# Seven-product units of the down projection: other places for their raw blocks, and splits written next to the loads

## The chip, the cores and the metric

The kernel runs on one core of one Trainium2 chip. The metric is the device time of one execution in microseconds; the time given is the median of several runs.

## The reference

One decoder block on x of 256 tokens by 2048 channels, in float32. Cut to what matters here:

```python
mix = token_mixers(x, w_in, ...)                 # GLA and forgetting attention, merged, projected by w_out
x = layer_norm(ALPHA * x + mix, ln1_g, ln1_b)
g = causal_dwconv(x @ w_gate, conv_w, conv_b)    # width 3
h = jax.nn.gelu(g) * (x @ w_up)                  # 256 x 5632
x = layer_norm(ALPHA * x + h @ w_down, ln2_g, ln2_b)
x = x + jax.nn.sigmoid(x @ w_ple_gate) * (p @ w_ple_proj)
```

The change concerns `h @ w_down`: 256 x 5632 times 5632 x 2048.

## The kernel before

All weights but a few pass through one stream of *units*, `wu[u]`, each 128 partitions by 2048 floats (1 MB). A float32 product is made of three products of float32r parts: an operand is *split* into a high part (`hi`, ScalarE's copy) and a low part (`lo`, VectorE's subtraction of the high part). `unit()` hands out the next unit's split parts and, before that, calls `prep()` until the units up to two ahead have been written into the program. `prep` loads a plain unit as two raw blocks of 128 x 1024 into a ring of 4 places (tag `raw`), splits them into `hi` and `lo` tiles (6 places each, tag `hi` and `lo`), and so feeds TensorE.

The down projection runs in two halves (`nh`), each over 22 units of two k-tiles and 1024 output columns, accumulating into four PSUM banks (`banks`, written dn in the trace). In a *plain* unit TensorE makes 24 products of 128 x 512 (`x_mm`, L300). Units listed in `DNW` (12 in the first half, 10 in the second; 1, 2, 4, 5, 7, 8, 10, 11, ...: mostly two, then a plain one) are *seven-product* units: `seven` (L321) multiplies by a Strassen-like scheme with 7 x 3 = 21 products, some into four more banks (`ms`, dn0m and dn1m). For it a unit needs

- block 0 and 1 of the unit (columns 0 to 1023) and block 3 (columns 1536 to 2047), split: `his`, `los`;
- four combinations of blocks, split, in two tiles `ts`: two were made beforehand, during the gate and up projections, by `combine` on VectorE, and stored in DRAM (`tsd`); the other two are made from blocks 0 and 1 in place, by subtracting the second stored combination (the *pair* subtraction, L151);
- sums of h, loaded into the free half of the first `hi` and `lo` tile by `sums[u]` (GpSimd's DMA queue, L1160 and L1161).

Wide tiles come from 15 places of 128 x 2048 (`s8`, tag S8): in this stage hT holds ten of them in the first half (hT0 to hT9, given back one by one in the second half as their last k-tile is used), the residual z2 two from the end of the first half on, the second LayerNorm's gain and offset two, and the rest serves the seven-product units' `raw` and `ts` tiles.

`prep_seven` loads blocks 0 and 1 into the first half of a wide tile `raw` and the two stored combinations into its second half, and block 3 into a ring place (`raws`). It splits block 3 and blocks 0 and 1 (L149) and makes the pair subtraction. The two tiles `ts` are split later by `split_seven` (L162): `unit()` calls it for the unit being handed out and the one after it, behind its calls of `prep()`.

The loads are issued by SyncE (SP), whose instructions stay in the order of the program (`manual_schedule`), so a load that waits for its place holds back those behind it. On ScalarE and VectorE the order is set by the compiler's planner, by priority (mostly the order of the program) among what its own clock holds ready; it also deals out the places. On the chip each engine then runs its queue strictly in that order.

Of the kernel before, what the change touches and what calls it, by code (L numbers as in the profile page):

```python
# [9 lines left out]
F32 = mybir.dt.float32  # L10
F32R = mybir.dt.float32r
# [3 lines left out]
ALU = mybir.AluOpType  # L15
# [4 lines left out]
P = 128  # L20
# [38 lines left out]
def tile_block(ctx: ExitStack, tc: tile.TileContext, wu, xw, wfv, wpp, xT_in, x_in, pT_in, wlr,  # L59
               chan, gnorm, lng, ident_in, mask_in, cmask_in, out):  # L60
    nc = tc.nc
# [4 lines left out]
    ring = ctx.enter_context(tc.tile_pool(name="ring", bufs=4))  # L66
# [14 lines left out]
    def s8(shape, dt=F32, name=None):  # L81
        t = big.tile([P, S8W], dt, tag="S8", name=name)
        n = int(np.prod(shape[1:]))
        t = t[:shape[0], :n]
        if len(shape) == 3:
            return t.rearrange("p (a b) -> p a b", b=shape[2])
        if len(shape) == 4:
            return t.rearrange("p (a b c) -> p a b c", b=shape[2], c=shape[3])
        return t

    def w_tile(tag, dt, name, u):
        if tag == "lo":
            return wide.tile([P, 1024], dt, tag=tag, name=name)
        o = 0 if u in XSTAT else HSTEP
        return wide.tile([P, WH], dt, tag=tag, name=name)[:, o:o + 1024]

    def t1(name):
        return sm.tile([P, 256], F32, tag="t1", bufs=6, name=name)
# [10 lines left out]
    def copy(o, i, scale=1.0):  # L109
        nc.scalar.activation(o, i, AF.Copy, bias=0.0, scale=scale)  # L110
# [14 lines left out]
    n_prep = [0]  # L125
    ready = {}

    sums, half, later = {}, {}, {}
    units7 = [DN0 + nh * (NF // 2) + i for nh in range(2) for i in DNW[nh]]
    tsi = {u: j for j, u in enumerate(units7)}  # L130
    tsd = dr.tile([len(units7), P, 1024], F32, name="tsd")

    def prep_seven(u):
        raw = s8([P, 2048], name=f"raw{u}")
        small = ring.tile([P, 1024], F32, tag="raw", bufs=4, name=f"raws{u}")[:, 0:512]
        nc.sync.dma_start(raw[:, 0:1024], wu[u, :, 0:1024])
        nc.sync.dma_start(small, wu[u, :, 1536:2048])
        nc.sync.dma_start(raw[:, 1024:2048], tsd[tsi[u]])
        his, los = [], []
        for h, b in enumerate((small, raw[:, 0:1024])):  # L140
            hi = w_tile("hi", F32R, f"hi{u}_{h}", u)
            lo = w_tile("lo", F32R, f"lo{u}_{h}", u)
            n = b.shape[1]
            his.append(hi)
            los.append(lo)
            if h == 0:
                sums[u](hi[:, 512:1024], lo[:, 512:1024])
            copy(hi[:, 0:n], b)
            nc.vector.tensor_tensor(lo[:, 0:n], b, hi[:, 0:n].bitcast(F32), ALU.subtract)  # L149
        pair = raw[:, 0:1024].rearrange("p (a b) -> p a b", b=512)  # L150
        nc.vector.tensor_tensor(pair, pair, raw[:, 1536:2048].unsqueeze(1).broadcast_to([P, 2, 512]),  # L151
                                ALU.subtract)
        half[u] = (his, los, raw)

    def split_seven(u):
        his, los, raw = half.pop(u)
        ts = []
        for h in (1, 0):
            t = s8([P, 2, 1024], F32R, name=f"ts{u}_{h}")
            e = raw[:, h * 1024:h * 1024 + 1024]  # L160
            copy(t[:, 0, :], e)
            nc.vector.tensor_tensor(t[:, 1, :], e, t[:, 0, :].bitcast(F32), ALU.subtract)  # L162
            ts.insert(0, t)
        ready[u] = (his, los, ts)

    def prep():
        u = n_prep[0]
        n_prep[0] += 1
        if u in sums:
            prep_seven(u)  # L170
            return
        his, los = [], []
        for h in range(2):
            raw = ring.tile([P, 1024], F32, tag="raw", bufs=4, name=f"raw{u}_{h}")
            nc.sync.dma_start(raw, wu[u, :, h * 1024:(h + 1) * 1024])
            hi = w_tile("hi", F32R, f"hi{u}_{h}", u)
            c = nc.scalar.activation(hi, raw, AF.Copy, bias=0.0, scale=1.0)  # L177
            if h == 0 and u > DN0:
                tc.keep_in_program_order(c)
            lo = w_tile("lo", F32R, f"lo{u}_{h}", u)  # L180

            def rest(lo=lo, raw=raw, hi=hi):
                return nc.vector.tensor_tensor(lo, raw, hi.bitcast(F32), ALU.subtract)  # L183

            if u in LATE_LO:
                later.setdefault(u, []).append(rest)
            elif u in PIN_LO:
                tc.keep_in_program_order(rest())
            else:
                rest()  # L190
            his.append(hi)
            los.append(lo)
        ready[u] = (his, los)
# [4 lines left out]
    def unit(ahead=3):  # L198
        u = n_used[0]
        n_used[0] += 1  # L200
        while n_prep[0] < min(NU, u + ahead):
            prep()
        for v in (u, u + 1):
            if v in half:
                split_seven(v)
        return ready.pop(u)


# [134 lines left out]
    def x_half(name, act, K, evac, pulls=0, head=0, tail=0, mid=None, done=None, end=None,  # L343
# [9 lines left out]
        def mm(i, w, toks, cs=(0, 1), part=None):  # L353
            for j in range(2):
                kt = 2 * i + j
                x_mm(banks, (w[0][j], w[1][j]), act[kt // 4][:, kt % 4, :], toks,
                     kt == 0, kt == K - 1, cs, part)

        us = [unit() for _ in range(head)]
        for t in range(2):  # L360
            for i, w in enumerate(us):
                mm(i, w, (t,))
        for i in range(head, n - tail):
            if i in ws:
                if i == ws[0]:
                    ms.extend(mmtile(f"{name}m{j}") if j % 2 == 0 else mxtile(f"{name}m{j}")
                              for j in range(4))
                seven(banks, ms, unit(), act, 2 * i, i == ws[0], i == ws[-1])
                if i == ws[-1]:
                    joined(ms)  # L370
            else:
                mm(i, unit(), (0, 1))
            pull(pulls)
            if mid is not None and i in mid:
                mid[i]()
# [121 lines left out]
    for t in range(2):  # L497
        for c, (o, n) in enumerate(fch):
            n = min(n, 1024 - o)
# [144 lines left out]
    for nm, dst, sc in (("fq", fq, P ** -0.5), ("fk", fk, 1.0)):  # L644
        if nm == "fk":
            mixers.append(fox_gen())
        for n in range(8):
            if nm == "fk" and n == 4:
                load_consts2()
            hi, lo = unit()  # L650
# [8 lines left out]
    for nm, dst, sc in (("q", gq, 1.0 / 16.0), ("k", gk, 1.0)):  # L659
        for n in range(8):  # L660
            hi, lo = unit()
            ps = mmtile(f"ps{nm}{n}")
            w_unit(ps, hi, lo, xT, range(16), True, True)
            h, c = n // 2, n % 2
# [163 lines left out]
    for n in range(32):  # L828
        hi, lo = unit()
# [15 lines left out]
    for n in range(16):  # L845
        hi, lo = unit()
# [343 lines left out]
    for n in range(NF):  # L1190
# [22 lines left out]
        u = t1("up")  # L1213
# [168 lines left out]
```

## Time and profile before

| | us |
|---|---|
| runs | 1665.45, 1667.3, 1673.34 (median 1667.3) |
| the profiled execution, its time | 1664.02 |
| its span, first to last instruction | 1662.2 |
| TensorE busy in the span | 1649.7 (99%) |
| VectorE, ScalarE busy | 1206.7 (73%), 871.6 (52%) |
| DMA, mean over the span | 230 GB/s |
| down projection, both halves | 1327.3 to 1554.5 |
| landing of a load from tsd, issue to landing, median | 8.1 |

A row of the table of windows gives the stretch, its length, then busy time and count for TensorE, its weight loads, VectorE, ScalarE and GpSimd, then the granted TensorE clock, the DMA share and GB/s. A row of a timeline gives start, duration, engine, line and operation, the tiles it writes and reads, and in brackets how long the engine was idle before it and what ended that. A row of waits gives who waited for whom, the total, the number of waits and the longest.

### The profile page before, as it was taken

How to read it: one execution, taken by the hardware profiler on the slowest of the kernel's cores; microseconds unless marked ns; L12 is line 12 of the kernel's file. 1: busy time of each engine (PE TensorE's matmuls, PEld its weight loads, DVE VectorE, ACT ScalarE, POOL GpSimd, SP SyncE). 2: the span in 40 equal slices, each digit the busy share in tenths (PEclk: the TensorE clock that was granted, in tenths of full speed). 3: DMA queues.
4: the chain of work that ended last, by engine and by line, in shares of the span. 5: the costliest groups of instructions: out<-in, count | busy, mean ns of one | idle time of the engine just before them, and what ended most of it. 6: DMA issues, size and time to landing. Idle time of an engine off the chain costs nothing.

```text
span 1662.2 us, 24249 instructions
## 1 busy us (share of the span) xinstructions
PE 1649.7 (99%) x8968; PEld 1431.4 (86%) x8968; DVE 1206.7 (73%) x1771; ACT 871.6 (52%) x1255; POOL 92.8 (6%) x213
## 2 busy tenths in 40 slices
PE   9999999999999999999999999999999999999998
PEld 9988888888888888888898888888888877877887
DVE  6666658768756657775688788888777778878774
ACT  6745445445556545444465455555555556456643
POOL 0000000000000000000010121111000111010000
PEclk9999999999999999999999999999999999999999
DMA  7765555555555555658647899988666588689364
GB/s 296 234 202 179 165 189 179 177 179 178 184 179 174 170 190 193 195 194 291 226 150 252 310 349 336 354 322 294 225 205 207 191 292 319 251 320 344 133 209 171
DMA packets 105799, 382.69 MB, mean 230 GB/s; under 512 B 12312, under 2 KB 13216, under 8 KB 104272
## 3 DMA queue, kind: packets, MB, share of 16 engines
q1 hardware_dynamic: 96144, 347.38, 61.1%
q0 software_dynamic: 9392, 33.57, 5.2%
q8 instruction: 70, 1.15, 0.3%
q14 instruction: 49, 0.40, 0.1%
q10 hardware_dynamic: 144, 0.20, 0.0%
HBM read 358.02 MB, written 23.08 MB: 229 GB/s over the span
## 4 chain that ended last, share of the span: by engine, by line
PE 94%; DMA 3%; DVE 1%; SPq 1%; issue 1%; ACT 0%; POOL 0%; DVEq 0%; ACTq 0%
PE psu L256 9%; PE psg L256 9%; PE psm L256 7%; PE dn L300 6%; PE gr L300 5%; PE gv L300 5%; PE wo L300 5%; PE pg L300 5%; PE psu L258 5%; PE psg L258 5%; PE psm L258 4%; PE psa L256 3%; PE fv L462 3%; DMA raw<-tsd 3%; PE psfq L256 2%; PE psfk L256 2%
## 5 line engine op out<-in xcount | busy, mean ns | idle before, releaser
L183 DVE TENSOR_TENSOR lo<-raw,hi 128x1024 fp32r<-128x1024 f32 x524 | 639.1, 1223 | 321.3 <-ACT hi L177 320.0
L177 ACT ACTIVATE hi<-raw 128x1024 fp32r<-128x1024 f32 x524 | 553.0, 1059 | 526.7 <-issue 138.6
L256 PE MATMUL psu<-x1T,hi 128*128 128x512 f32 x688 | 236.0, 389 | 0.0
L256 PE MATMUL psg<-x1T,hi 128*128 128x512 f32 x672 | 230.6, 389 | 0.0
L258 PE MATMUL psu<-x1T,lo 128*128 128x256 f32 x688 | 190.2, 276 | 0.0
L258 PE MATMUL psg<-x1T,lo 128*128 128x256 f32 x672 | 185.9, 277 | 0.0
L256 PE MATMUL psm<-xT,hi 128*128 128x512 f32 x512 | 175.8, 391 | 0.0
L256 PEld LDWEIGHTS psu<-x1T,hi 128*128 128x128 f32 x688 | 129.3, 188 | 26.4
L256 PEld LDWEIGHTS psg<-x1T,hi 128*128 128x128 f32 x672 | 126.3, 188 | 25.9
L258 PE MATMUL psm<-xT,lo 128*128 128x256 f32 x512 | 141.7, 277 | 0.0
L258 PEld LDWEIGHTS psu<-x1T,lo 128*128 128x128 f32 x688 | 129.2, 188 | 0.0
L258 PEld LDWEIGHTS psg<-x1T,lo 128*128 128x128 f32 x672 | 126.1, 188 | 0.3 <-DVE lo L183 0.3
L256 PEld LDWEIGHTS psm<-xT,hi 128*128 128x128 f32 x512 | 96.2, 188 | 19.6
L300 PE MATMUL dn<-hi,hT 128*128 128x512 f32 x352 | 98.1, 390 | 0.0
L258 PEld LDWEIGHTS psm<-xT,lo 128*128 128x128 f32 x512 | 96.2, 188 | 0.1
L256 PE MATMUL psa<-oT,hi 128*128 128x512 f32 x256 | 87.8, 389 | 0.0
L300 PEld LDWEIGHTS dn<-hi,hT 128*128 128x128 f32 x352 | 66.0, 188 | 13.6
L300 PE MATMUL gv<-hi,xT 128*128 128x512 f32 x256 | 72.3, 394 | 0.0
L300 PE MATMUL gr<-hi,xT 128*128 128x512 f32 x256 | 72.2, 394 | 0.0
L258 PE MATMUL psa<-oT,lo 128*128 128x256 f32 x256 | 70.8, 276 | 0.0
L300 PE MATMUL wo<-hi,mT 128*128 128x512 f32 x256 | 69.9, 390 | 0.0
L300 PE MATMUL pg<-hi,x2T 128*128 128x512 f32 (+1 forms) x256 | 68.3, 378 | 0.0
(307 smaller groups left out, 2960.6 us busy)
## 6 DMA issues: line engine op xcount, KB each, us to landing
raw<-in_wu_dram SPq DMA_DIRECT2D x546, 512.0 KB, 4.7
comb<-in_wu_dram SPq DMA_DIRECT2D x22, 768.0 KB, 8.9
tsd<-comb POOLq DMA_DIRECT2D x22, 512.0 KB, 7.7
raw<-tsd SPq DMA_DIRECT2D x22, 512.0 KB, 8.1
fvraw<-in_wfv_dram SPq DMA_DIRECT2D x15, 524.0 KB, 7.8
raws<-in_wu_dram SPq DMA_DIRECT2D x22, 256.0 KB, 7.1
hi<-hsd POOLq DMA_DIRECT2D x22, 256.0 KB, 5.4
lo<-hsd POOLq DMA_DIRECT2D x22, 256.0 KB, 6.0
```

What stands on the lines that cost most here:

```text
L177: c = nc.scalar.activation(hi, raw, AF.Copy, bias=0.0, scale=1.0)
L183: return nc.vector.tensor_tensor(lo, raw, hi.bitcast(F32), ALU.subtract)
L256: nc.tensor.matmul(ps, lhsT=hi[i // 8 if hoff == 0 else 0][:, w0 % 1024:w0 % 1024 + P], rhs=a[:, kt % 4, :], start=first and i == 0, stop= ...
L258: nc.tensor.matmul(ps[:, 256:512], lhsT=lo[i // 8 if hoff == 0 else 0][:, w0 % 1024:w0 % 1024 + P], rhs=a[:, kt % 4, 0:256], start=False, ...
L300: nc.tensor.matmul(bs[j][:, 0:m], lhsT=x, rhs=v[:, o:o + m], start=first and i == 0, stop=last and i == 2)
L462: nc.tensor.matmul(fbk[t][c][:, 0:n], lhsT=x, rhs=w[:, o:o + n], start=kt == 0 and i == 0, stop=kt == 15 and i == 2)
```

## The change

For a seven-product unit, blocks 0 and 1 are loaded into a ring place (`low`, 128 x 1024) and the stored combinations and block 3 into a wide place (`top`, 128 x 1536), in the order blocks 0 and 1, combinations, block 3. `split_seven` and its calls in `unit()` go away; the two `ts` tiles are split at the end of `prep_seven`, the untouched second one first.

```diff
     def prep_seven(u):
-        raw = s8([P, 2048], name=f"raw{u}")
-        small = ring.tile([P, 1024], F32, tag="raw", bufs=4, name=f"raws{u}")[:, 0:512]
-        nc.sync.dma_start(raw[:, 0:1024], wu[u, :, 0:1024])
-        nc.sync.dma_start(small, wu[u, :, 1536:2048])
-        nc.sync.dma_start(raw[:, 1024:2048], tsd[tsi[u]])
-        his, los = [], []
-        for h, b in enumerate((small, raw[:, 0:1024])):
+        low = ring.tile([P, 1024], F32, tag="raw", bufs=4, name=f"raw{u}")
+        top = s8([P, 1536], name=f"top{u}")
+        nc.sync.dma_start(low, wu[u, :, 0:1024])
+        nc.sync.dma_start(top[:, 0:1024], tsd[tsi[u]])
+        nc.sync.dma_start(top[:, 1024:1536], wu[u, :, 1536:2048])
+        his, los, ts = [], [], []
+
+        def split(hi, lo, b):
+            copy(hi, b)
+            nc.vector.tensor_tensor(lo, b, hi.bitcast(F32), ALU.subtract)
+
+        def sevenths(h, b):
+            t = s8([P, 2, 1024], F32R, name=f"ts{u}_{h}")
+            split(t[:, 0, :], t[:, 1, :], b)
+            ts.insert(0, t)
+
+        for h, b in enumerate((top[:, 1024:1536], low)):
...
-            copy(hi[:, 0:n], b)
-            nc.vector.tensor_tensor(lo[:, 0:n], b, hi[:, 0:n].bitcast(F32), ALU.subtract)
-        pair = raw[:, 0:1024].rearrange("p (a b) -> p a b", b=512)
-        nc.vector.tensor_tensor(pair, pair, raw[:, 1536:2048].unsqueeze(1).broadcast_to([P, 2, 512]),
+            split(hi[:, 0:n], lo[:, 0:n], b)
+        pair = low.rearrange("p (a b) -> p a b", b=512)
+        nc.vector.tensor_tensor(pair, pair, top[:, 512:1024].unsqueeze(1).broadcast_to([P, 2, 512]),
                                 ALU.subtract)
-        half[u] = (his, los, raw)
-
-    def split_seven(u):
...
+        sevenths(1, top[:, 0:1024])
+        sevenths(0, low)
         ready[u] = (his, los, ts)
...
         while n_prep[0] < min(NU, u + ahead):
             prep()
-        for v in (u, u + 1):
-            if v in half:
-                split_seven(v)
         return ready.pop(u)
```

More of the change, by code (lines that the diff above doesn't have):

```diff
@@ L126, in tile_block @@
     ready = {}
-    sums, half, later = {}, {}, {}
+    sums, later = {}, {}
     units7 = [DN0 + nh * (NF // 2) + i for nh in range(2) for i in DNW[nh]]
@@ L147, in prep_seven @@
                 sums[u](hi[:, 512:1024], lo[:, 512:1024])
-            copy(hi[:, 0:n], b)
-            nc.vector.tensor_tensor(lo[:, 0:n], b, hi[:, 0:n].bitcast(F32), ALU.subtract)
-        pair = raw[:, 0:1024].rearrange("p (a b) -> p a b", b=512)
-        nc.vector.tensor_tensor(pair, pair, raw[:, 1536:2048].unsqueeze(1).broadcast_to([P, 2, 512]),
+            split(hi[:, 0:n], lo[:, 0:n], b)
+        pair = low.rearrange("p (a b) -> p a b", b=512)
+        nc.vector.tensor_tensor(pair, pair, top[:, 512:1024].unsqueeze(1).broadcast_to([P, 2, 512]),
                                 ALU.subtract)
-        half[u] = (his, los, raw)
-    def split_seven(u):
[L156 to L163, printed above, removed]
+        sevenths(1, top[:, 0:1024])
+        sevenths(0, low)
         ready[u] = (his, los, ts)
```

## The prediction, made before the changed kernel ran

> **What bounds the kernel now.** I first read the page's busy table, then cut the span into stages with the table of windows, to see where TensorE is not busy.
>
> ```profile
> PE 1649.7 (99%) x8968; PEld 1431.4 (86%) x8968; DVE 1206.7 (73%) x1771; ACT 871.6 (52%) x1255; POOL 92.8 (6%) x213
> ```
>
> ```profile
> 14.00:835.00 821.00, 820.95 (x4504) 717.11 (x4503) 545.79 (x849) 421.26 (x643) 10.28 (x15) 1.00 0.59 196
> 875.00:1327.30 452.30, 452.26 (x2660) 400.78 (x2660) 363.83 (x573) 234.41 (x346) 53.01 (x136) 1.00 0.78 277
> 1327.30:1554.50 227.20, 221.09 (x969) 181.12 (x968) 182.37 (x185) 125.97 (x137) 21.70 (x41) 1.00 0.83 301
> ```
>
> TensorE is busy for 1649.7 of 1662.2 us, so 12.5 us of idle time is all that any reordering can win, in the whole kernel. The change touches only the down projection. That is the stage from 1327.3 to 1554.5, where TensorE is busy 221.09 of 227.20 us at a granted clock of 1.00: 6.11 us idle. The two long stages ahead of it have next to none. Next I looked for those 6.11 us in TensorE's timeline, by the idle times that it prints behind an instruction:
>
> ```profile
> 1366.14 0.39 PE L321 MATMUL dn0m<-ts,hi 128*128 128x512 f32 x1
> 1368.18 0.50 PE L321 MATMUL dn0m<-ts,hi 128*128 128x512 f32 x1 [1.65 <-DVE ts L162]
> 1400.08 0.50 PE L321 MATMUL dn0m<-ts,hi 128*128 128x512 f32 x1 [1.69 <-DVE ts L162]
> 1484.13 0.51 PE L321 MATMUL dn1m<-ts,hi 128*128 128x512 f32 x1 [1.33 <-DVE ts L162]
> 1501.62 0.50 PE L321 MATMUL dn<-lo,hi 128*128 128x512 f32 x1 [0.83 <-DVE lo L149]
> 1506.16 0.50 PE L321 MATMUL dn1m<-ts,hi 128*128 128x512 f32 x1 [0.62 <-DVE ts L162]
> ```
>
> These five make 6.12 us, all of it. By the order of the units they belong to unit 7 (1.65) and unit 13 (1.69) of the first half, and unit 7 (1.33) and unit 11 (0.83 + 0.62) of the second. Four of the five wait for the DVE half of a split of a combination (L162). What DVE and ACT did ahead of the first one:
>
> ```profile
> 1359.46 1.23 DVE L149 TENSOR_TENSOR lo<-raw,hi 128x1024 fp32r<-128x1024 f32 x1 [3.86 <-ACT hi L110]
> 1360.60 0.69 DVE L149 TENSOR_TENSOR lo<-raws,hi 128x512 fp32r<-128x512 f32 x1
> 1361.20 1.22 DVE L151 TENSOR_TENSOR raw<-raw 128x1024 f32<-128x1024 f32 x1
> 1362.34 1.22 DVE L162 TENSOR_TENSOR ts<-raw,ts 128x1024 fp32r<-128x1024 f32 x1
> 1364.02 1.23 DVE L149 TENSOR_TENSOR lo<-raw,hi 128x1024 fp32r<-128x1024 f32 x1 [0.47 <-ACT hi L110]
> 1365.17 0.68 DVE L149 TENSOR_TENSOR lo<-raws,hi 128x512 fp32r<-128x512 f32 x1
> 1365.77 1.22 DVE L151 TENSOR_TENSOR raw<-raw 128x1024 f32<-128x1024 f32 x1
> 1366.90 1.22 DVE L162 TENSOR_TENSOR ts<-raw,ts 128x1024 fp32r<-128x1024 f32 x1
> ```
>
> ```profile
> 1362.93 1.06 ACT L110 ACTIVATE hi<-raw 128x1024 fp32r<-128x1024 f32 x1 [1.45 <-PE dn L300]
> 1364.41 1.99 ACT L110 ACTIVATE ts<-raw 128x1024 fp32r<-128x1024 f32 x2
> ```
>
> The first four DVE rows are unit 7: its two raw splits, its pair subtraction, its first combination split. The fifth to seventh rows are unit 8, whose data had only just landed; the eighth is unit 7's second split, for which TensorE stands still until 1368.18. Its input was finished by the third row, at 1362.4. It ran 4.5 us later because both queues had unit 8's instructions ahead of it. So this stall is an order on two in-order engines, not a lack of engine time (DVE is busy 182 of 227 us in the stage).
>
> **The change part by part.** Nothing is added to or removed from any engine: per seven-product unit there remain three loads of 512, 512 and 256 KB, four copies on ACT and five subtractions on DVE of the same shapes, and TensorE's 21 products.
>
> (a) Both combination splits stand in the program right behind the unit's raw splits, instead of one unit later. With the row durations: unit 7's pair subtraction ends at 1362.4, its first split at 1363.5, and ACT's copy for the second (about 1.0 us, half of the 1.99) fits beside that. Then the second split runs 1363.5 to 1364.7. TensorE wants it at 1366.14 + 0.23 = 1366.4. Slack 1.7 us, so 1.65 us go. The chain is the same for unit 13 (1.69) and for unit 7 of the second half (1.33). Together 4.67 us. What is late next is unit 8: it gains what unit 7 no longer interleaves, so its splits end no later than now, while TensorE reaches it 1.65 us earlier. Unit 8's last split would follow its pair subtraction at 1365.77 by 1.1 and 1.1 us, ending near 1369.2; TensorE starts that unit now at 1368.18 + 1.26 = 1369.44 and wants the split 15 products later: 1369.44 + 15 x 0.227 - 1.65 = 1371.2 (0.227 us a product: a plain unit's 24 take 5.44 us in the chain). It holds.
>
> Bounds of (a): nothing, if the order on the queues stays, and 4.67 us. I take 4.67, since the ready time lies 4.5 us before the run time.
>
> (b) Places. The stage has 15 wide places. hT holds 10, so 5 remain in the first half; the second half starts with 3, since z2 takes two, and wins one back with every second unit. Before, a unit needs one for its raw tile until both splits are done. After, the tile `top` is let go by the pair subtraction and the first split, one split (1.2 us) earlier; but the two `ts` places are wanted earlier too. The load queue shows what decides now:
>
> ```profile
> 1351.38 0.33 SPq L136 DMA_DIRECT2D raw<-in_wu_dram  x1
> 1352.76 0.36 SPq L136 DMA_DIRECT2D raw<-in_wu_dram  x1
> 1354.45 0.70 SPq L138 DMA_DIRECT2D raw<-tsd  x1
> 1355.25 1.12 SPq L175 DMA_DIRECT2D raw<-in_wu_dram  x2
> ```
>
> ```profile
> SPq L136 <- DVE ts L162: 53.6, 10, 11.8
> SPq L136 <- PE dn0m L321: 28.1, 6, 9.1
> ```
>
> ```profile
> 1354.45 10.10 DMA raw<-tsd
> 1374.37 5.44 PE dn L300 x24
> ```
>
> SP waits 53.6 us in total for a split to free a wide place and 28.1 us for TensorE to free one. Then two sevens and a plain unit leave within 5 us (1351.38 to 1356.4), 3.5 MB at once, and unit 8's combination takes 10.10 us to land. After the change `low` needs no wide place, so its 512 KB can leave while SP still waits for one, and the burst shrinks. Gain in TensorE time: none by itself in the first half, where (a) has the stalls already; it is reserve.
>
> (c) The ring of 4 places. `raws` left it after its own subtraction (1360.60 + 0.69 = 1361.3). `low` stays until the unit's last split, near 1364.7 by (a): 3.4 us longer. Behind it on SP stand the plain unit's two loads (L175) and all later loads. Unit 9's left at 1355.25 and TensorE reaches it at about 1374: 18.7 us. Landing takes 11.1 us at most in this half (the row below), and two copies and two subtractions of 1.1 to 1.2 us take 3.5 us with overlap; 4.1 us are left. So 3.4 us more are covered, barely; without that cover it would cost up to 3.4 us in each of eight pairs. I take nothing, as a pair uses 2 ring places and its plain unit 2, which is exactly 4.
>
> ```profile
> DMA to landing us min/median/max: 3.9/8.2/11.1
> ```
>
> ```profile
> 1490.00:1507.30 17.30, 15.85 (x68) 12.24 (x67) 12.16 (x13) 9.11 (x10) 2.12 (x4) 1.00 1.02 412
> 1357.90:1374.60 16.70, 15.05 (x67) 12.15 (x66) 13.78 (x13) 10.89 (x13) 2.13 (x4) 1.00 0.91 328
> ```
>
> (d) Unit 11 of the second half is another case: 1.45 us. That stretch moves 17.3 x 412 = 7.1 MB at a DMA share of 1.02; with the two 1 MB gain loads among it, the queues are full. Without its stall it would be 15.85 us and need 450 GB/s, more than any stretch shows, unless loads move ahead of it. They partly do: unit 10's load leaves now just as unit 7's delayed split ends, and that comes earlier by (a):
>
> ```profile
> 1482.85 1.23 DVE ts L162
> 1484.08 0.02 issue
> 1484.10 0.33 SPq L136
> ```
>
> The gain ends: nothing, if the stretch cannot go faster than it does, and 1.45. I take the middle, 0.7, as neither row is nearer.
>
> The Trainium skill, DMA: Bandwidth & Descriptors, "Where 436 GB/s comes from", gives about 358 GB/s from HBM for a core whose neighbour streams too, and 435 for the fabric. By 358 the pair around unit 7 (16.7 x 328 = 5.5 MB), shortened by its stall to 15.05 us, would need 15.3 us and give 0.3 us back per pair. The trace does not agree with that limit: 412 GB/s over 17.3 us.
>
> (e) The third block is now the last of the three loads and the combinations the second: 0.4 us later and earlier (the issue of one load). The block's product opens the unit, but a unit lands ahead of TensorE by more than that. Nothing.
>
> (f) The start of the stage and the second half's first sevens, where places are fewest:
>
> ```profile
> 1323.47 0.33 SPq L136 DMA_DIRECT2D raw<-in_wu_dram  x1
> 1453.73 0.33 SPq L136 DMA_DIRECT2D raw<-in_wu_dram  x1
> 1455.06 0.43 SPq L136 DMA_DIRECT2D raw<-in_wu_dram  x1
> ```
>
> ```profile
> 1453.89 1.36 PE dn L321 x6
> ```
>
> ```profile
> 1468.81 0.39 PE L321 MATMUL dn<-hi 128*128 128x512 f32 x1
> ```
>
> Unit 2's load leaves when the first x1T place is free (1323.47). If unit 1's two splits, now first in the program, take the first two x1T places (a quarter of a 5.4 us unit apart), `top` of unit 2 leaves 2.7 us later, at 1326.2. TensorE reaches that unit at 1327.4 + 5.44 + 4.76 = 1337.6, and the load lands in 6 to 8 us: covered. In the second half, unit 5's combinations leave after 1455.06; if unit 4's splits take the place first, they wait for unit 2's TensorE work (1453.89 + 15 x 0.227 = 1457.3), 2.2 us later, and after 8 to 10 us of landing and 4.5 us of splits stand ready within a microsecond of need (unit 5 starts at 1468.8). A gain is excluded here, as TensorE has no idle time at these units; between nothing and 1 us of loss I take 0.4, nearer to nothing, because the place may as well go to SP first, as it does now.
>
> Sum: 4.67 + 0.7 - 0.4 = 5.0 us gained. The profiled execution took 1664.02 us, 1.8 us of it outside the span, so 1659.0; the median of the three runs is 1667.3, 3.3 us above the profiled one, so 1662.3.
>
> **The rivals.**
> 1. *The order stays.* The queues' order comes from a planner that fills an engine with whatever it believes ready. If it believes unit 8 landed with unit 7, ACT copies unit 8's raw block (1362.93) in the microsecond in which it waits for unit 7's pair subtraction, and the second split still hangs on unit 8's landing. For it: that very row. Against: only one copy of 1.06 us could slip in, and `low` of unit 8 now leaves earlier. Gain 0 to 2.5: 1665 to 1667.3.
> 2. *The places run short, the side of a loss.* If the planner lets the combination splits of a pair's first unit take the places that TensorE frees, `top` of the second waits for that first split. Counted from the start of TensorE on the preceding pair: first load at 3.4, landed at 13.5, split by 18, second load then, landed at 26 to 28, split at 29 or later, needed at 14.96 + 4.76 + 2.0 = 21.8. That is 7 us of stall in such a pair. One such pair eats the whole gain (6.1 us); two of the eight end 8 us slower (1675), all eight 50 us. Against: SP stands at the place's door before the data of that split have landed, so it should be served first. It decides from 1.8 us a pair.
> 3. *DMA is the bound.* Unit 11's 1.45 us stays and a little moves to the next pairs: gain 3 to 4.7, 1663 to 1664. For it: the share of 1.02 at unit 11; against: the other pairs move 328 GB/s and less. By the Trainium skill's 358 GB/s (DMA: Bandwidth & Descriptors, the section above) up to eight pairs would give back 0.3 us each, 2.4 us in all, within this rival's chance.
>
> **How the numbers follow.** This kernel's runs spread by 0.5% (1665.45 to 1673.34), so 0.5%, 8.3 us, is about what can be told from no change; the stage's idle 6.11 us is 0.37%. A faster verdict would need luck in the runs: 0.05. Forecast, gain 4 to 6.1: 0.45. Rival 3: 0.15. Rival 1: 0.16. A loss under 8.3 us (rival 2 in one pair, or the ring): 0.08. A larger loss: 0.11. So faster 0.05, same 0.84, slower 0.11. The range is from 1658 (all 6.1 us, and runs 3 us better) to 1670 (no gain, 0.16% of spread), leaving out the losses.
>
> **What would show it.** Right: no L162 idle in TensorE's timeline at units 7 and 13; DVE's rows for one unit in one piece (two L149, pair, two splits); TensorE idle in the stage below 2 us; `low` leaving on SP ahead of its `top` by microseconds. Wrong: SP waiting on `top` for a split of the same pair (rival 2), a raw split of the next unit ahead of the second combination split (rival 1), or plain loads waiting for `low` places (c).

## The result, and the profile after

The changed kernel takes 1658.8 us (median of 20 runs, 1656.8 to 1667.8), the kernel before beside it 1665.2 us (20 runs, 1660.9 to 1675.5). The ratio is 0.9962, with an interval of 0.9945 to 0.9979: 6.3 us faster, where 5.0 us were forecast, and inside the 0.5% called "no change that can be told" in the prediction. The profiled execution of the changed kernel took 1661.2 us (span 1659.5). One thing is needed to read the absolute times below: some executions of every kernel here, the one before included, take about 9 us longer, as TensorE makes fewer products in the gate and up stage (1870 instead of 1925 between 1000 and 1327.3 us, at a granted clock of 1.00 in both), and in one set of runs, that with the late gain loads, nearly all did; so kernels are compared by their ratio to the kernel before in the same set.

The busy table of the changed kernel, then its stages by the table of windows (columns: busy us and instructions of PE, PEld, DVE, ACT and POOL, granted clock, DMA share, GB/s):

```profile
PE 1649.8 (99%) x8968; PEld 1430.5 (86%) x8968; DVE 1208.2 (73%) x1771; ACT 873.1 (53%) x1255; POOL 93.1 (6%) x213
```

```profile
875.00:1327.30 452.30, 452.26 (x2660) 399.94 (x2659) 363.74 (x572) 234.32 (x345) 53.05 (x136) 1.00 0.78 277
1327.30:1550.00 222.70, 222.17 (x979) 182.91 (x978) 184.15 (x186) 127.23 (x137) 21.68 (x41) 1.00 0.87 306
```

The work is the same to the instruction (8968, 1771, 1255, 213), and the stage ahead is the same to 0.01 us. In the down projection TensorE is now idle 0.53 us, where it was 6.11. What is left is seen in the two waits of TensorE from there on:

```profile
PE ptl L888 <- DVE z L882: 2.6, 1, 2.6
PE dn L318 <- DVE lo L143: 0.5, 1, 0.5
```

No wait for a split of a combination is left. The 0.5 us is unit 11 of the second half. The 2.6 us is the wait for the first normalized tile of LN2 (the second LayerNorm) at the end of the stage, which was 0.6 us. So in this execution one wait grew as the others went. It is not a fixed price of the change: a second profile of the same kernel, further down, has 1.15 us there. DVE's timeline around unit 7 of the first half shows the new order:

```profile
1356.47 1.23 DVE L143 TENSOR_TENSOR ts<-top,ts 128x1024 fp32r<-128x1024 f32 x1 [1.58 <-ACT ts L110]
1357.61 0.69 DVE L143 TENSOR_TENSOR lo<-top,hi 128x512 fp32r<-128x512 f32 x1
1358.21 1.22 DVE L160 TENSOR_TENSOR raw<-raw,top 128x1024 f32<-128x1024 f32 x1
1359.62 1.23 DVE L143 TENSOR_TENSOR lo<-raw,hi 128x1024 fp32r<-128x1024 f32 x1 [0.19 <-ACT hi L110]
1360.77 1.22 DVE L143 TENSOR_TENSOR ts<-raw,ts 128x1024 fp32r<-128x1024 f32 x1
1361.90 1.22 DVE L160 TENSOR_TENSOR raw<-raw,top 128x1024 f32<-128x1024 f32 x1
```

The first three rows and the fifth are unit 7: a combination, the third block, the pair, the other combination, which ends at 1362.0 instead of 1368.1. Unit 7's other raw split stands ahead of them, at 1353.66. The fourth row is unit 8's raw split, which the planner still slips in ahead of unit 7's last one. That is what rival 1 named, and unit 7 is not in the one piece that the prediction expected. TensorE opens unit 7 only at 1362.69 and takes 15 products before that split, 3.4 us, so it wants it at 1366.1: 4 us of slack, and the row costs nothing.

### The profile page after: what moved, and what is told of

It reads as the page before. It is cut to its first block, busy times and chain, and to the rows that moved or that the text cites. A ratio compares the mean times of both kernels' runs of the same rounds, so it can differ in the third digit from the quotient of the medians.

```text
span 1659.5 us, 24269 instructions
## 1 busy us (share of the span) xinstructions
PE 1649.8 (99%) x8968; PEld 1430.5 (86%) x8968; DVE 1208.2 (73%) x1771; ACT 873.1 (53%) x1255; POOL 93.1 (6%) x213
## 3 DMA queue, kind: packets, MB, share of 16 engines
q8 instruction: 70, 1.15, 0.3%
## 4 chain that ended last, share of the span: by engine, by line
PE 94%; DVE 2%; DMA 2%; ACT 1%; issue 1%; SPq 0%; POOL 0%; ACTq 0%; DVEq 0%
PE psu L253 9%; PE psg L253 9%; PE psm L253 7%; PE gr L297 5%; PE gv L297 5%; PE dn L297 5%; PE wo L297 5%; PE psu L255 5%; PE psg L255 5%; PE pg L297 4%; PE psm L255 4%; PE psa L253 3%; PE fv L459 3%; PE dn L318 2%; PE dn0m L318 2%; PE psfq L253 2%
```

## The experiments

Four theories stood. A: the order of the splits is the whole gain, and places and loads add nothing. Its rival: the gain comes from the places, since loads leave earlier. C: the ring place that `low` holds makes the wait at LN2. D: unit 11's wait comes from the two gain loads that start beside it.

**The order alone.**

```
 # the kernel before, prep_seven
         half[u] = (his, los, raw)
+        split_seven(u)
 # unit()
-        for v in (u, u + 1):
-            if v in half:
-                split_seven(v)
```

> The places of before (blocks 0 and 1 with the combinations in a wide place, block 3 in a ring place), but both combination splits stand right behind the unit's raw splits. Theory A (the gain is the order of the splits on VectorE and ScalarE): TensorE's idle time in the down projection falls from 6.1 us to under 2 us, no stall behind a combination split at units 7 and 13 of the first half, time 4 to 6 us under before. Theory B (the gain is the places, which let the 512 KB of blocks 0 and 1 leave SP earlier): idle time stays at 4 us or more, time less than 2 us under before. Theory C (a ring place held by blocks 0 and 1 until the last split is what delays the second LayerNorm): here block 3 leaves the ring early, so the wait of 2.6 us for the normalised z goes back to under 1 us and this kernel is 1 to 2 us faster than after.

Measured: 1658.2 us beside 1664.0 for the kernel before, ratio 0.9961 (0.9942 to 0.9980). The places, the ring and the loads are those of before, and the time is that of the whole change. In DVE's timeline unit 7 is now in one piece (the first four rows; the last is unit 8's):

```profile
1358.50 1.23 DVE L149 TENSOR_TENSOR lo<-raw,hi 128x1024 fp32r<-128x1024 f32 x1 [1.94 <-ACT hi L110]
1359.64 0.68 DVE L149 TENSOR_TENSOR lo<-raws,hi 128x512 fp32r<-128x512 f32 x1
1360.25 1.22 DVE L151 TENSOR_TENSOR raw<-raw 128x1024 f32<-128x1024 f32 x1
1361.38 2.50 DVE L163 TENSOR_TENSOR ts<-raw,ts 128x1024 fp32r<-128x1024 f32 x2
1364.61 1.23 DVE L149 TENSOR_TENSOR lo<-raw,hi 128x1024 fp32r<-128x1024 f32 x1 [0.73 <-ACT hi L110]
```

Its stalls, as TensorE's waits and the two halves of the stage:

```profile
PE dn1m L319 <- ACT ts L110: 1.9, 1, 1.9
PE ptl L889 <- DVE z L883: 1.0, 1, 1.0
PE dn1m L319 <- DVE ts L163: 0.5, 1, 0.5
```

```profile
1327.30:1442.00 114.70, 114.70 (x508) 94.95 (x508) 92.54 (x96) 65.30 (x72) 12.02 (x23) 1.00 0.89 311
1442.00:1550.00 108.00, 105.58 (x464) 86.48 (x463) 90.97 (x90) 60.73 (x66) 9.61 (x18) 1.00 0.84 305
```

The first half has no idle time. The second has 2.4 us in this execution, 1.9 of it at one product of unit 2, which the planner set among those of unit 1, ahead of the copy it needs. The LN2 wait is 1.0 us here, between the 0.6 of before and the 2.6 of the change, and the run time is that of the change. A second profile of this kernel (it was run again for the last comparison) has neither the 1.9 us nor the 1.0: there TensorE is idle 1.2 us in the stage and waits 0.6 us at LN2. Waits of this size come and go between executions of one kernel.

**The places alone.** The new places and loads, the splits late as before.

```
 # the changed kernel, prep_seven
-        sevenths(1, top[:, 0:1024])
-        sevenths(0, low)
-        ready[u] = (his, los, ts)
+        half[u] = (his, los, low, top)
 # and split_seven(v) called from unit() again, over low and top
```

> The places and load order of after, but the combination splits are written one unit later, as in before. Theory A: the second combination split of unit 7 again stands behind raw splits of unit 8, TensorE idles 3 us or more in the down projection, time within 2 us of before. Theory B: idle time under 2 us, time 4 to 6 us under before, like after.

Measured: 1681.2 us, ratio 1.0097 (1.0066 to 1.0129), six runs. The three shortest took 1674.5 to 1676.6 us, and even these lie some 11 us above the kernel before (1664.0). No theory had that. SyncE's waits and its timeline show what it is:

```profile
SPq L136 <- DVE ts L165: 63.4, 9, 10.7
```

```profile
1361.81 0.73 SPq L138 DMA_DIRECT2D top<-in_wu_dram  x1
1362.58 2.23 SPq L178 DMA_DIRECT2D raw<-in_wu_dram  x2
1375.25 0.33 SPq L136 DMA_DIRECT2D raw<-in_wu_dram  x1
```

After the plain unit's two loads the ring of four is full: two `low`, two plain. The next `low` stands at the head of SyncE's queue until a split that is now one unit late frees a place, 10.7 us at worst, and all later loads stand behind it. TensorE then waits at the other end:

```profile
PE dn L303 <- DVE z L972: 5.1, 1, 5.1
PE dn0m L324 <- DVE ts L165: 2.9, 4, 0.8
```

The first of these is the start of the second half, where the products wait for a residual addition; LN2 costs another 4.2 us of wait in this profile. So the new places are no gain, and with late splits they are a loss: they need the new order.

**The order of the loads.** Block 3 ahead of the combinations, in the changed kernel.

```
-        nc.sync.dma_start(top[:, 0:1024], tsd[tsi[u]])
         nc.sync.dma_start(top[:, 1024:1536], wu[u, :, 1536:2048])
+        nc.sync.dma_start(top[:, 0:1024], tsd[tsi[u]])
```

> After, with block 3 loaded ahead of the stored combinations again. Both theories: no change to after beyond 1 us, since a unit lands microseconds ahead of TensorE; if the order of the three loads matters, the combinations land 0.4 us later and the time rises by 1 us or more.

Measured: 1662.8 us, ratio 0.9990 (0.9974 to 1.0005): 4 us of the gain are gone. It is not one stall but many small ones, and beside them the ring comes free later. SyncE's wait for a split to free a place of the ring, in this kernel and in the changed one (41.6 us in the changed kernel's second profile):

```profile
SPq L136 <- DVE ts L143: 65.4, 16, 9.0
```

```profile
SPq L136 <- DVE ts L143: 42.1, 16, 6.5
```

And TensorE's waits grew from 0.5 us to 3.5 us in the stage, and at LN2 to this:

```profile
PE ptl L888 <- DVE z L882: 3.3, 1, 3.3
```

The converse was run in the order-only kernel, whose `raws` leaves the ring early: combinations loaded ahead of block 3.

```
 # the order-only kernel
-        nc.sync.dma_start(small, wu[u, :, 1536:2048])
         nc.sync.dma_start(raw[:, 1024:2048], tsd[tsi[u]])
+        nc.sync.dma_start(small, wu[u, :, 1536:2048])
```

> The order alone, with the combinations loaded ahead of block 3 as in the changed kernel. If the order of the three loads matters by itself (e3_load_order lost some 4 us to the changed kernel by the reverse step), this kernel is 2 to 4 us faster than the order alone; if the loss came from the planner's other order of splits or from the wide place held longer, it is within 1 us of it or slower.

Measured: 1660.1 us beside 1658.6 for order alone in the same set of runs (ratios to before 0.9971, 0.9952 to 0.9990, and 0.9961, 0.9937 to 0.9984). There it does not help. So the order of the loads was worth something only together with `low` in the ring. That it works through the ring is argued from SyncE's waits, not shown: DVE's order of splits changed with it, and the two were not taken apart.

**The wait at LN2.** In the changed kernel DVE did this ahead of it:

```profile
1546.13 2.46 DVE L183 TENSOR_TENSOR lo<-raw,hi 128x1024 fp32r<-128x1024 f32 x2 [2.90 <-ACT hi L177]
1548.50 0.68 DVE L966 TENSOR_TENSOR z<-z,dn 128x512 f32<-128x512 f32 x1
```

The residual additions (L966), from which LN2 starts, stand behind two low parts of a later plain unit, whose load came late (6.67 us by the chain, 1539.49 to 1546.16). The next kernel writes those low parts behind the first LN2 tile.

```
-            if u in LATE_LO:
+            if u in LATE_LO + END_LO:          # END_LO = (268,)
 # done2, behind ln_out(..., t)
+        if t == 0:
+            for u in END_LO:
+                for rest in later[u]: rest()
```

> After, but VectorE's low parts of the first gate unit of the per-layer embedding (unit 268) are written behind the second LayerNorm of the first 128 tokens, so that the residual additions and statistics no longer stand behind them. Theory A: TensorE's wait of 2.6 us for the normalised z falls to 0.6 us as in before, and the time is 1.5 to 2 us under after, unless the moved low parts are late for the gate (a wait on lo at its start). Rival: the residual additions wait for something else, and the 2.6 us stay.

Measured: 1659.3 us, ratio 0.9968 (0.9947 to 0.9988): no different from the change, where 1.5 to 2 us less were expected. TensorE's timeline:

```profile
1551.63 1.09 PE L889 MATMUL ptl<-ident,z 128*128 128x128 f32 x8 [0.63 <-DVE z L883]
1565.14 0.66 PE L889 MATMUL ptl<-ident,z 128*128 128x128 f32 x4 [1.85 <-ACT lny L896]
```

The first wait fell from 2.56 to 0.63, and 1.85 us stand 13 us later, at the second tile, which the changed kernel's profile had not. In this profile the wait was moved, not removed. How much of either this kernel's one difference made stays open, since the changed kernel without it has 2.56 us in one profile and 1.15 in the other.

**The gain loads later.** `mid2a`, which starts the loads of the two gains, called at step 15 instead of step 8 of the second half, in three kernels.

```
-    ..., {8: mid2a, NF // 2 - 5: mid2b}), done2, ws=DNW)
+    ..., {15: mid2a, NF // 2 - 5: mid2b}), done2, ws=DNW)
```

In the kernel before:

> Before, with the two 1 MB loads of the second LayerNorm's gain and offset issued behind unit 15 of the second half instead of unit 8. Theory D (unit 11 of the second half stands still because those 2 MB fill the DMA queues ahead of its own loads): its 1.45 us go, the other 4.67 us stay, time 1 to 2 us under before. Rival: unit 11 stands still for the same reason as unit 7, the order of the splits; then the stall stays within 0.5 us and the time is that of before.

Measured: 1670.0 us beside 1673.3, ratio 0.9976 (0.9954 to 0.9999). Unit 11's two waits (0.83 and 0.62) are gone, and in the second half this is the only row left:

```profile
1477.46 0.50 PE L321 MATMUL dn1m<-ts,hi 128*128 128x512 f32 x1 [1.32 <-DVE ts L162]
```

But this row is unit 4, which did not wait before, and the waits of unit 7 are gone in both halves, the first of them (1.65 us) ahead of anything that the later gain loads touch. Unit 13's stays, with 1.45 us. Which units wait differs from one execution to the next, so this pair alone does not show theory D. In the changed kernel:

> After, with the gain loads behind unit 15. Theory D: the wait of 0.5 us at unit 11 goes, the loads behind it land earlier, and the chain of loads and splits that leads from there to the second LayerNorm has slack again: the wait of 2.6 us falls to 1 us or less and the time is 1 to 3 us under after. Rival: the chain is set by ring places and VectorE, not by these loads: the 2.6 us stay, or grow since the gain loads now stand next to the embedding's loads, and the time is the same or 1 us more.

Measured: 1667.7 us, ratio 0.9964 (0.9944 to 0.9984). TensorE is never idle in the stage up to 1550, the LN2 wait is 0.9 us, and the ratio is still that of the change without it (0.9962):

```profile
1327.30:1442.00 114.70, 114.70 (x520) 95.36 (x519) 92.67 (x95) 66.62 (x74) 13.90 (x26) 1.00 0.83 290
1442.00:1550.00 108.00, 108.00 (x478) 89.44 (x477) 93.06 (x96) 61.51 (x68) 10.64 (x20) 1.00 0.89 311
```

```profile
PE ptl L888 <- DVE z L882: 0.9, 1, 0.9
```

The second profile of the changed kernel, with the gain loads where they were, shows the same, so none of this can be put down to the gain loads:

```profile
1327.30:1550.00 222.70, 222.70 (x996) 184.79 (x995) 185.59 (x191) 129.39 (x141) 24.55 (x46) 1.00 0.85 299
```

```profile
PE ptl L888 <- DVE z L882: 1.1, 1, 1.1
```

In the order-only kernel:

> The order alone (e1_order_only) with the gain loads behind unit 15. Theory D: its stall of 0.5 us at unit 11 goes; time 0 to 1.5 us under e1_order_only.

Measured: 1667.3 us, ratio 0.9953 (0.9933 to 0.9973), the lowest of that set, and so it was run again. This kernel is the best evidence for theory D: order alone waits at unit 11 in both of its profiles (0.5 and 0.6 us), and with late gains neither profile has a wait there. The second profiles of the two, each with its longest wait for a split or copy of a combination:

```profile
PE dn1m L319 <- DVE ts L163: 0.6, 1, 0.6
```

```profile
PE dn1m L319 <- ACT ts L110: 0.7, 1, 0.7
```

The second of these stands at unit 2. Four profiles make theory D likely; in time it is worth nothing that these runs can tell.

**`low` out of the ring at once.** The changed kernel, with the pair subtraction writing into a wider `top`, so that the ring place is free one split earlier, and the last split taken from there.

```
-        top = s8([P, 1536], name=f"top{u}")
+        top = s8([P, 2048], name=f"top{u}")
-        nc.vector.tensor_tensor(pair, pair, top[...], ALU.subtract)
+        nc.vector.tensor_tensor(dst, pair, top[...], ALU.subtract)    # dst: top[:, 1024:2048]
-        sevenths(0, low)
+        sevenths(0, top[:, 1024:2048])
```

> After, but the pair subtraction writes its result into the wide place (over block 3, once that is split), so that blocks 0 and 1 leave the ring two splits earlier and the wide place stays until the last split, as in before. Theory C (the ring place held until the last split costs time through the loads queued on SP): SP's waits for ring places behind a combination split go, TensorE's wait at the second LayerNorm falls under 1.5 us, and the time is 1 to 3 us under after. Rival (the wide places bind, not the ring): SP waits as long for the wide place, and the time is the same or more than after.

Measured: 1670.9 us beside 1667.7 for the changed kernel with late gains and 1673.3 for the one before; ratio 0.9979 (0.9960 to 0.9999). SyncE's waits:

```profile
SPq L136 <- DVE top L161: 34.5, 12, 6.9
SPq L137 <- PE dn0m L319: 29.2, 8, 5.0
```

The ring's wait is a little shorter (42.1 and 41.6 in the changed kernel's two profiles), the wait for a wide place (L137) rises from 19.4 and 15.8 to 29.2, and the LN2 wait is 1.6 us. The place was taken from where it was just as scarce. Theory C, that the ring makes the LN2 wait, is not borne out: with the ring's wait shorter the LN2 wait lies between the 2.56 and the 1.15 of the change. The run is no clean test of it, as the wide places grew scarcer at the same time.

**The best ones side by side.** The changed kernel, order alone, and order alone with late gains once more, in one set of runs.

> The changed kernel again, on the same chip as the three beside it, so that they can be compared with it directly. Ratio to before 0.996 as in its first comparison; TensorE's wait for the normalised z between 0.6 and 3 us, by what DMA does in that execution.

> The order alone, again, beside the changed kernel. Theory A (the order is all of the gain): within 1.5 us of the changed kernel. Theory B (the places and the earlier loads carry part of it): 2 us or more behind the changed kernel.

> The order alone with the gain loads behind unit 15, beside the changed kernel: its profile had 0.35 us of idle time in the down projection and no wait for the normalised z, so 1 to 3 us under the changed kernel if that holds in most executions; the same if the profile was a lucky one.

Measured: 1658.9 (ratio 0.9963, 0.9942 to 0.9984), 1658.6 (0.9961, 0.9937 to 0.9984) and 1658.2 us (0.9962, 0.9941 to 0.9982). They are level. No version here beats the change by more than can be measured, and hardly one could: 6.1 us was all of TensorE's idle time in the stage, in the one profile of before.

## Why the prediction was right, by its own steps

The whole, 5.0 us forecast and 6.3 measured, is the forecast case (4 to 6.1 us), a little over its end. That the two are so near is in part luck: the interval of the measurement runs from 3.5 to 9.2 us, and of the smaller terms below one was put at nothing that is worth 4 us and one was taken off that did not come. The prediction had no term at all for LN2 behind the stage. The runs of before fell lower than the first three had shown (median 1665.2 instead of 1667.3), and so did those after.

(a) The order: right in mechanism and size, and shown alone. Order alone gives all of the gain, to within the 3 us or so of the interval, and the waits at units 7 and 13 are gone. The second combination split of unit 7 ended at 1362.0, earlier than the 1364.7 worked out, as its loads left earlier: on SyncE's queue `low` at 1347.02 and the combinations at 1349.90, where they had left at 1351.38 and 1352.22. `low` left 2.9 us ahead of its `top`, as forecast.

(b) The places: no gain by themselves, right; but "reserve" was too kind. With late splits they cost some 11 us.

(c) The ring: "nothing" held for the change, but not for the ring by itself. The mechanism named there, loads queued behind a place that `low` holds, is the largest wait of SyncE after the change (42.1 us in 16 waits, where before these loads waited for a wide place instead), and with late splits it is a loss of 11 us. In the change the cover held: no unit of the stage but unit 11 waits. At its end, in the profiled execution, a late load put two low parts ahead of the residual additions; the second profile has 1.15 us of wait there. What this end costs in the median was not isolated.

(d) Unit 11: 0.7 of 1.45 us was taken, 0.9 came (0.53 left), and all of it in the second profile; the gain loads are the likely cause. The stall shrank without a higher rate of the DMA: 17.3 us of that place now move 375 GB/s at a share of 0.98, where it was 412 at 1.02.

```profile
1482.00:1499.30 17.30, 16.77 (x72) 12.83 (x71) 10.29 (x11) 6.90 (x9) 3.12 (x6) 1.00 0.98 375
```

So rival 3 did not come: loads moved ahead of the gains, as the step allowed. Unit 10's first load left 5.0 us ahead of them (1474.81 and 1479.84), where it had been 1.6 (1484.10 and 1485.68). That 412 GB/s went over the 358 quoted in the prediction is no contradiction: that figure was given there for a core whose neighbour streams too, and this kernel ran on one core. (e) The order of the loads, put at nothing: 4 us in the changed kernel. This is the step most in error. It counted the issue of one load (0.4 us) against the slack of the unit's own data, and nothing for the units behind, whose loads wait 65.4 us for the ring in the reverse order and 42.1 in the changed kernel. (f) The shortage of places, 0.4 us: no wait stands there, at the start of either half. At the start of the stage what it described did happen, `top` of unit 2 leaving at 1326.14 where 1326.2 was worked out, and the slack covered it. That its place came only with TensorE's next release, where it had left at 1323.47 before, suggests that SyncE was not served first there, as the prediction expected against rival 2. Rival 1's slip-in happened and cost nothing; rival 2, wide places running short, did not come in the change, and came mildly with the wider `top`.

The two profiled spans differ by less than the medians, 2.7 us, and the profiled execution of the changed kernel is 2.4 us slower than its median. TensorE's timelines give the way: at the first LN2 transposes the changed kernel is 4.74 us ahead (1553.11 against 1557.85), at the next stage's first product 3.2 (1558.99 against 1562.19). The 1.6 us between lie in the same 11 products, in the chains of before and of after:

```profile
1558.95 2.53 PE dn L300 x11
```

```profile
1554.20 4.11 PE dn L297 x11
```

In the second profile of the changed kernel the same products took no longer than before, so this loss belongs to the one execution and not to the change:

```profile
1561.07 2.52 PE dn L297 x11
```

## What to carry to other kernels

When an engine stands still for a result whose input was ready several microseconds before, look at what the in-order queue ran in between: putting the late half of a step behind its own first half costs no work and gave here all of the gain that could be measured. A buffer that is moved from one pool to another takes the wait along: look at which queue stands at the new pool's door and what is queued behind it, before calling the move free. And when an engine is at 99%, a wait taken away at one place may be met again a few microseconds on, as at LN2, so the stage's idle time is about the most that any of it can bring. One profile is one execution: the LN2 wait was 2.56 us in one profile of the changed kernel and 1.15 in the other, so a wait that only one profile shows is not yet a price of the change.

## What the runs showed of the hardware that was not expected

The granted clock of TensorE fell for some microseconds after some waits, and not after others of the same length. In the changed kernel, after the 2.56 us wait that ended at 1553.11:

```profile
1550.00:1553.00 3.00, 0.55 (x3) 0.13 (x1) 2.22 (x7) 0.36 (x1) 0.56 (x1) 1.00 0.59 213
1553.00:1556.00 3.00, 2.89 (x14) 2.46 (x15) 2.38 (x6) 2.88 (x5) 0.00 (x0) 0.73 0.00 0
1556.00:1559.00 3.00, 3.00 (x13) 2.44 (x12) 1.55 (x2) 2.97 (x7) 0.00 (x0) 0.70 0.08 26
1559.00:1562.00 3.00, 3.00 (x16) 2.48 (x16) 2.97 (x8) 0.56 (x1) 0.00 (x0) 1.00 0.48 154
```

Its second profile, with a wait of 1.15 us at the same place, kept 1.00. The kernel with the places alone showed it after its 5.07 us wait, and the one with block 3 first after 3.34 us:

```profile
1459.80:1463.00 3.20, 3.13 (x7) 2.34 (x8) 3.20 (x7) 0.00 (x0) 0.00 (x0) 0.51 0.47 156
```

```profile
1560.00:1565.00 5.00, 5.00 (x19) 3.99 (x18) 3.06 (x7) 4.76 (x9) 0.00 (x0) 0.69 0.15 52
```

The kernel with late low parts showed it after 1.85 us (1563.29 to 1565.14), although TensorE had been busy without a gap just before:

```profile
1559.00:1562.00 3.00, 3.00 (x18) 2.42 (x17) 2.66 (x8) 2.76 (x6) 0.55 (x1) 1.00 0.04 14
1565.00:1570.00 5.00, 4.86 (x18) 4.01 (x19) 4.32 (x8) 5.00 (x12) 0.00 (x0) 0.66 0.55 176
```

The 1.92 us wait of order alone, which ended at 1444.71, left it at 1.00, and so did the two of 1.65 and 1.69 us in the kernel before:

```profile
1444.70:1448.00 3.30, 3.29 (x14) 2.74 (x15) 3.30 (x4) 0.00 (x0) 0.00 (x0) 1.00 0.86 292
```

So the length of the wait does not decide it by itself: 1.85 us did it and 1.92 us did not. What else counts, no run here separates. The Trainium skill, TensorE: Matmul & The Clock Gate, "What's actually happening", puts the clock back to half after one idle window of about 3.4 us, which runs free of the kernel. The waits of 5.07 and 3.34 us agree with it or nearly do; 2.56 and 1.85 us are less than the page says. In the profiled execution of the changed kernel the 2.56 us wait cost about 1.6 us more than itself, by the 11 products above.
